# Summing the modulation vectors by 32x32 turns on VectorE and one small matmul, with the w_mod tiles in three buffers

## The chip, the cores and the metric

The kernel runs on one core of one Trainium2 chip. The metric is the device time of one execution in microseconds (us). A core has several engines that work side by side: TensorE (matrix products; PE in the profile, PEld its loading of weights), VectorE (DVE), ScalarE (ACT), GpSimd (POOL) and SyncE (SP), whose queue here issues all the DMA transfers from the main memory to the core's own.

## The reference

Two layers work on 256 latent tokens and 256 context tokens of width 1024. What matters here is the modulation: each layer makes six vectors of 1024 numbers out of the conditioning vector, once for the latent tokens (from c) and, where they are still needed, once for the context tokens (from c_ctx).

```
mod   = silu(c)     @ w_mod[l] + b_mod[l]
mod_c = silu(c_ctx) @ w_mod[l] + b_mod[l]
sh1, sc1, gt1, sh2, sc2, gt2 = split(mod, 6)
...
h = rms_norm(x, g_norm1) * (1 + sc1) + sh1          # then w_in, three mixers, three gates
x = x + gt1 * (merged branches @ w_o)
x = x + gt2 * (square(relu((rms_norm(x, g_norm2) * (1 + sc2) + sh2) @ w_ff1)) @ w_ff2)
```

w_mod[l] is 1024 x 6144 numbers of 4 bytes. It is as large a matrix as the others, but it is multiplied by two vectors only.

## The kernel before

**The main work.** All activations lie with the feature on the partition. Every big matrix comes from memory in tiles of 1 MB (`ffL_raw`, `gateL_raw` and so on, two buffers). ScalarE rounds a tile to its high part (`whi`, L384), VectorE computes the low part (`wlo`, L385), and TensorE multiplies in three passes: high by high (L473), low by high (L476) and high by low (L478). In the feed-forward part of layer 1 the same three passes stand in L1110 to L1112. The stages of a layer follow each other: norm 1, u, conv, Fourier, qkv, gate (with the attention beside it), ag, wo, ff.

**The modulation beside it.** At the start, shift and scale of norm 1 of layer 0 are computed by TensorE (`mod_start`). All other vectors are made in the background by a generator, `mod_steps`, whose list holds (layer, vector j, number of streams): four vectors with two streams in layer 0, two with two streams in layer 1, four with one stream in layer 1. For each half of a vector (512 columns) it asks for four tiles of w_mod of 512 KB (`modr`, L298: 256 rows x 512 columns, two row blocks of 128). For each row block and stream VectorE does one step: it multiplies the 128 x 512 block by the conditioning numbers of these 128 rows, one for each partition, and adds the product to an accumulator `acc` (L349 for the first, L351 for the others). After 16 steps two accumulators are full: either the same half for both streams, or both halves for one stream.

**The finish.** Each accumulator then still has to be summed over its 128 partitions, and the sums have to be turned so that the feature lies on the partition. That is `mod_finish`, and it is called 16 times: 8 for the four vectors of layer 0, 4 for the two first ones of layer 1, 4 for the last ones. Before the change it does, for each pair of accumulators:

- three empty steps (W1), then four matmuls of 32 equal rows of ones by 256 columns of an accumulator (L308); each puts 256 sums on 32 partitions of one PSUM tile, all 32 rows alike
- a copy of that 128 x 256 tile to SBUF by ScalarE (L313)
- two empty steps (W2), then two 128 x 128 transposes by TensorE (L318) to a PSUM tile of the kind `aux`, which the attention uses too
- two additions of the bias by VectorE (L321), which write the vectors to `modT`

**What sets the order.** `fm`, the function of the three passes, calls `mods.tick()` after each of its 128-row blocks of the contraction. A tick adds the stage's rate (RATES: 0.6 in gate, 1.3 in ag, 0.4 in wo, 0.8 in ff), and each time a whole step is due, one step of the generator is written into the program. `mod_need` writes at once all steps that are left until a vector is ready: before wo for vectors 2, 3 and 4 of layer 0, and in the first block of ff for vector 5. `mods.drain` writes all that is left before the last projection of layer 0. The instructions of the modulation are pinned among each other by `keep_in_program_order`; the others are put in order for each engine by a scheduler that simulates the timeline when the program is built. An instruction with no pin can so be placed ahead of others that were written before it, once its buffer is free. Each engine then takes its list strictly in order.

**The start.** Two tiles of the kind `modr` serve at first as a place for weights of `w_in` (`start_raw`, L501); the first w_mod tile of the generator comes when one of them is free.

Of the kernel before, what the change touches and what calls it, by code (L numbers as in the profile page):

```python
# [1 line left out]

# [6 lines left out]
F32 = mybir.dt.float32  # L9
F32R = mybir.dt.float32r  # L10
AF = mybir.ActivationFunctionType
ALU = mybir.AluOpType
AX = mybir.AxisListType
PSUM = bass.MemoryType.PSUM

P = 128
D = 1024
# [13 lines left out]
W_INIT, W_RMS = 6, 6  # L31
MLAG = 1
LAG = 2
W1, W2 = 3, 2
RATES = [0.6, 1.3, 0.4, 0.8]
AR = [1.3, 0.8]

# [2 lines left out]
def hybrid_block_kernel(  # L40
# [7 lines left out]
    nc = tc.nc  # L48
    V = nc.vector
    A = nc.scalar  # L50
    G = nc.gpsimd
    PE = nc.tensor

    const = ctx.enter_context(tc.tile_pool(name="const", bufs=1))
# [4 lines left out]
    tiny = ctx.enter_context(tc.tile_pool(name="tiny", bufs=4))  # L59
    psum = ctx.enter_context(tc.tile_pool(name="psum", bufs=4, space=PSUM))  # L60
    paux = ctx.enter_context(tc.tile_pool(name="paux", bufs=3, space=PSUM))
    pmod = ctx.enter_context(tc.tile_pool(name="pmod", bufs=1, space=PSUM))
# [4 lines left out]
    def nm(s):  # L67
        uid[0] += 1
        return f"{stage[0]}_{s}_{uid[0]}"
# [4 lines left out]
    def scratch(shape=(P, 512), dt=F32):  # L74
        return scr.tile(list(shape), dt, tag="scr", name=nm("scr"))

    def small(shape, tag, dt=F32, bufs=4):
        return tiny.tile(shape, dt, tag=tag, name=nm(tag), bufs=bufs)

    def bank(shape=(P, 512)):  # L80
        return psum.tile(list(shape), F32, tag="mm", name=nm("mm"))

    def aux(shape=(P, 512)):
        return paux.tile(list(shape), F32, tag="aux", name=nm("aux"))

    def raw_tile():
        return rpool.tile([P, 2048], F32, tag="raw", name=nm("raw"))

    class Ring:
# [6 lines left out]
        def next(self):  # L96
            self.i += 1
            return self.t[:, self.lo + self.i % self.n, :]
# [31 lines left out]
    ident = const.tile([P, P], F32, tag="ident", name="ident")  # L130
    make_identity(nc, ident)
    ones = const.tile([P, P], F32, tag="ones", name="ones")
    G.memset(ones, 1.0)
    mhalf = const.tile([P, 1], F32, tag="mhalf", name="mhalf")
    G.memset(mhalf, -0.5)
    cT = scratch((P, KT, 32))
# [10 lines left out]
    prm = []  # L147
# [38 lines left out]
    def accs(streams):  # L186
        t = const.tile([P, 4, 512], F32, tag="kT", name=nm("acc"))[:, 0, :]
        return [Acc(s * S, S, t) for s in streams]
# [62 lines left out]
    modT = [const.tile([P, 48, 2], F32, tag=f"modT{l}", name=f"modT{l}") for l in range(DEPTH)]  # L251
# [40 lines left out]
    def mod_loads(todo):  # L292
        for l, j, ns in todo:
            for h in range(2):
                for k2 in range(KT // 2):
                    r = tiny.tile([P, 2, 512], F32, tag="modr", name=nm("modr"), bufs=2)
                    c0 = j * D + h * 512
                    nc.sync.dma_start(r, w_mod[l, k2 * 256 : (k2 + 1) * 256, c0 : c0 + 512]  # L298
                                      .rearrange("(k p) n -> p k n", p=P))
                    yield l, j, ns, h, k2, r  # L300

    def mod_finish(accs, dsts, l):

        ps = pmod.tile([P, 256], F32, tag="mod", name=nm("mod"))
        for _ in range(W1):
            yield
        for g in range(4):
            tc.keep_in_program_order(PE.matmul(  # L308
                ps[32 * g : 32 * g + 32, :], ones[:, 0:32],
                accs[g // 2][:, (g % 2) * 256 : (g % 2 + 1) * 256], start=True, stop=True,  # L310
            ))
        sb = scratch()[:, :256]
        A.copy(sb, ps)  # L313
        for _ in range(W2):
            yield
        tp = aux((P, 2, P))
        for e in range(2):
            tc.keep_in_program_order(PE.transpose(tp[:, e, :], sb[:, e * P : (e + 1) * P], ident))  # L318
        tv = tp.rearrange("p e (g r) -> p g e r", r=32)[:, :, :, 0]
        for i, (f, s) in enumerate(dsts):  # L320
            V.tensor_tensor(  # L321
                modT[l][:, f : f + 4, s].rearrange("p (g e) -> p g e", e=2),
                tv[:, 2 * i : 2 * i + 2, :],
                prm[l][:, f : f + 4].rearrange("p (g e) -> p g e", e=2), op=ALU.add,
            )
        yield

    ready = set()
# [4 lines left out]

    def mod_steps(todo):
        loads = mod_loads(todo)
        cur = next(loads, None)
        accs, dsts = [], []
        while cur is not None:
            l, j, ns, h, k2, r = cur
            cur = next(loads, None)  # L340
            if k2 == 0:
                for s in range(ns):
                    accs.append(small([P, 512], "acc", bufs=2))
                    dsts.append((j * 8 + h * 4, s))
            for kk in range(2):
                for s in range(ns):
                    a, w = accs[s - ns], cs2[:, s, 2 * k2 + kk : 2 * k2 + kk + 1]
                    if k2 + kk == 0:
                        v = V.tensor_scalar(a, r[:, kk, :], w, None, op0=ALU.mult)  # L349
                    else:  # L350
                        v = V.scalar_tensor_tensor(a, r[:, kk, :], w, a, op0=ALU.mult, op1=ALU.add)  # L351
                    tc.keep_in_program_order(v)
                    yield
            if k2 == KT // 2 - 1 and len(accs) == 2:
                yield from mod_finish(accs, dsts, l)
                accs, dsts = [], []
                if h == 1:
                    ready.add((l, j))
# [129 lines left out]
    def residual(f, ps, gt, streams, acc):  # L488
        for s in streams:
# [5 lines left out]
            if acc is not None:  # L495
# [2 lines left out]

    start_raw = [raw_tile(), raw_tile()]
    start_raw = [[r[:, i * 1024 : (i + 1) * 1024] for i in range(2)] for r in start_raw]  # L500
    start_raw.append([tiny.tile([P, D], F32, tag="modr", name=nm("modr"), bufs=2)  # L501
                      for _ in range(2)])

    def start_weights(i):
# [41 lines left out]
    for l in range(DEPTH):  # L546
        last = l == DEPTH - 1
        ns = 1 if last else 2
# [15 lines left out]
        if l == 0:  # L564
# [31 lines left out]
            for i in range(3):  # L596
                go(KT - 1, i, i + 1)
            mods.set(mod_steps(
                [(0, j, 2) for j in range(2, 6)] + [(1, 1, 2), (1, 0, 2)]
                + [(1, j, 1) for j in range(2, 6)]  # L600
# [15 lines left out]
        for ft in range(2):  # L616
            t = scratch()
# [15 lines left out]
        for ft in range(2):  # L633
# [4 lines left out]
            t = scratch()  # L638
# [31 lines left out]
        for tt in range(nt):  # L670
            ps = aux((P, 2, 256))
# [17 lines left out]
        for ft in range(2):  # L689
            ps = aux()  # L690
# [111 lines left out]
        for ci, c0 in ((2, OFF_K), (0, OFF_Q), (1, OFF_Q + 256)):  # L802
            ch = plain(w_in[l], 0, c0, (V, G) if last else (V, V)).prep()
            for tt in range(4 if ci == 2 else nt):
                ps = bank((P, 256))
                tk = slice(tt * P, (tt + 1) * P)
                for kt in range(KT):
                    wh, wl = ch.at(kt, 0, 256)
                    a, b = hh[:, kt, tk], hl[:, kt, tk]
# [122 lines left out]
        for j in range(4):  # L932
# [5 lines left out]
            for o in range(2):  # L938
                f = 2 * j + o
# [42 lines left out]
        acc = accs(streams)  # L982
# [50 lines left out]
        for b in range(nblk):  # L1033
            subs = []
            hot = None
            for q in range(2):
                hid = bigt([P, 2, per, T])
                subs.append(hid)
                for j in range(per // 2):
# [12 lines left out]
                    for o in range(2):  # L1052
                        t = scratch()[:, :T]
# [20 lines left out]
            if nr == 1:  # L1074
                if final and not last:
                    mods.drain()
                    acc = accs(streams)
# [17 lines left out]
            else:  # L1095

                nk = 2 * per
                for h in range(2):
# [14 lines left out]
                    for tt in range(2):  # L1113
                        t = scratch()
# [51 lines left out]
```

## Time and profile before

| what | value |
|---|---|
| three timed runs | 1146.95, 1144.39, 1149.06 us; median 1146.95 us |
| the profiled execution | 1148.35 us, its span 1146.5 us |
| granted TensorE clock | 0.996 |
| VectorE busy | 779.6 us (68%) |
| ScalarE busy | 504.4 us (44%) |
| DMA, all queues | 180.03 MB, 157 GB/s on the mean |

The span runs from the first to the last instruction; 1.85 us of the execution lie around it. A group of instructions is shown with its line, its engine, its operation, what it writes and reads, its shape and count; then its busy time, the mean of one in ns, and the engine's idle time before it with what ended it. In the timeline each row has a start and a length in us, and equal neighbours are merged. The length of a matmul is longer than the distance to the next one, because matmuls are pipelined: what one costs is read from the distances of the starts. A TensorE product of plain 4-byte numbers stands as two records, one of its transposes as one.

### The profile page before, as it was taken

The numbers are of one execution on the slowest core, as the hardware profiler recorded it, in microseconds if no ns is written. First come the engines' busy times: TensorE is split into PE (matmuls) and PEld (weight loads), VectorE is DVE, ScalarE is ACT, GpSimd is POOL, SyncE is SP. The second block draws the span as 40 slices with busy tenths as digits, with TensorE's granted clock in tenths as the row PEclk, the third lists the DMA queues.
The fourth block names the chain that finished last, engine by engine and source line by source line (L and its number), as shares of the span: only waits on it lengthen the run. The fifth ranks groups of instructions, "written<-read, shape, count | busy, mean of one in ns | idle before, by whom it ended". The sixth has DMA issues, their size and how long they took to land.

```text
span 1146.5 us, 17789 instructions
## 1 busy us (share of the span) xinstructions
PE 1127.0 (98%) x7075; PEld 983.9 (86%) x7075; DVE 779.6 (68%) x1444; ACT 504.4 (44%) x896; POOL 50.6 (4%) x54
## 2 busy tenths in 40 slices
PE   7899999999999999999999999999999999999998
PEld 6689887887787998878888888899999999988986
DVE  4577775568878876766746664778886567756754
ACT  4345544443332454143134135244666456754752
POOL 0002100000000100000000000043300000000000
PEclk9999999999999999999999999999999999999999
DMA  9933322225655243655456664515434465656653
GB/s 279 295 97 100 107 78 92 82 85 147 202 175 179 91 162 117 196 184 165 146 168 202 217 209 145 199 61 175 139 111 129 131 207 178 184 182 186 184 184 111
DMA packets 156796, 180.03 MB, mean 157 GB/s; under 512 B 5260, under 2 KB 126504, under 8 KB 156712
## 3 DMA queue, kind: packets, MB, share of 16 engines
q1 hardware_dynamic: 156712, 178.88, 50.1%
q8 instruction: 56, 0.92, 0.3%
q14 instruction: 28, 0.23, 0.1%
HBM read 177.81 MB, written 1.05 MB: 156 GB/s over the span
## 4 chain that ended last, share of the span: by engine, by line
PE 88%; DVE 4%; DMA 4%; SPq 2%; ACT 1%; issue 1%; POOL 1%; DVEq 0%; ACTq 0%; POOLq 0%
PE ffL_mm L473 12%; PE ffL_mm L476 12%; PE ffL_mm L478 12%; PE gateL_mm L478 5%; PE gateL_mm L473 5%; PE gateL_mm L476 5%; PE agL_mm L476 3%; PE agL_mm L473 3%; PE agL_mm L478 3%; PE ffL_mm L1112 3%; PE ffL_mm L1111 3%; PE ffL_mm L1110 3%; PE woL_mm L476 2%; PE woL_mm L478 2%; PE woL_mm L473 2%; SPq L105 2%
## 5 line engine op out<-in xcount | busy, mean ns | idle before, releaser
L384 ACT CAST ffL_whi<-ffL_raw 128x1024 fp32r<-128x1024 f32 x128 | 134.4, 1052 | 218.9 <-PE ffL_mm L478 164.3
L385 DVE TENSOR_TENSOR ffL_wlo<-ffL_raw,ffL_whi 128x1024 fp32r<-128x1024 f32 x127 | 155.0, 1222 | 99.3 <-ACT ffL_whi L384 99.1
L473 PE MATMUL ffL_mm<-woL_big,ffL_whi 128*128 128x258 f32 (+2 forms) x544 | 171.0, 329 | 0.0
L476 PE MATMUL ffL_mm<-woL_big,ffL_wlo 128*128 128x258 f32 (+2 forms) x544 | 170.5, 327 | 0.0
L478 PE MATMUL ffL_mm<-woL_big,ffL_whi 128*128 128x258 f32 (+2 forms) x544 | 133.2, 328 | 0.0
L473 PEld LDWEIGHTS ffL_mm<-woL_big,ffL_whi 128*128 128x128 f32 x544 | 103.1, 190 | 10.2 <-issue 1.6
L476 PEld LDWEIGHTS ffL_mm<-woL_big,ffL_wlo 128*128 128x128 f32 x544 | 103.1, 190 | 8.9 <-issue 0.4
L351 DVE SCALAR_TENSOR_TENSOR ffL_acc<-ffL_modr,cs,ffL_acc 128x512 f32<-128x512 f32 x126 | 90.4, 747 | 24.4 <-DMA ffL_modr<-in_w_mod_dram 23.4
L473 PE MATMUL ffL_mm<-ffL_big,ffL_whi 128*128 128x512 f32 (+1 forms) x288 | 105.4, 368 | 0.0
L476 PE MATMUL ffL_mm<-ffL_big,ffL_wlo 128*128 128x512 f32 (+1 forms) x288 | 104.9, 367 | 0.0
L478 PEld LDWEIGHTS ffL_mm<-woL_big,ffL_whi 128*128 128x128 f32 x544 | 91.0, 190 | 8.7
L478 PE MATMUL ffL_mm<-ffL_big,ffL_whi 128*128 128x512 f32 (+1 forms) x288 | 85.1, 367 | 0.0
L473 PEld LDWEIGHTS ffL_mm<-ffL_big,ffL_whi 128*128 128x128 f32 x288 | 54.3, 189 | 10.6 <-issue 2.1
L476 PEld LDWEIGHTS ffL_mm<-ffL_big,ffL_wlo 128*128 128x128 f32 x288 | 54.3, 189 | 9.1 <-issue 0.4
L385 DVE TENSOR_TENSOR gateL_wlo<-gateL_raw,gateL_whi 128x1024 fp32r<-128x1024 f32 x40 | 48.8, 1221 | 19.3 <-ACT gateL_whi L384 19.1
L478 PEld LDWEIGHTS ffL_mm<-ffL_big,ffL_whi 128*128 128x128 f32 x288 | 53.2, 189 | 8.7
L384 ACT CAST gateL_whi<-gateL_raw 128x1024 fp32r<-128x1024 f32 x40 | 42.0, 1051 | 22.0 <-PE gateL_mm L478 18.2
L476 PE MATMUL gateL_mm<-n1L_big,gateL_wlo 128*128 128x512 f32 x128 | 50.7, 396 | 0.0
L473 PE MATMUL gateL_mm<-n1L_big,gateL_whi 128*128 128x512 f32 x128 | 50.5, 396 | 0.0
L1110 PE MATMUL ffL_mm<-ffL_whi,ffL_big 128*128 128x512 f32 x128 | 49.9, 390 | 0.0
L1111 PE MATMUL ffL_mm<-ffL_wlo,ffL_big 128*128 128x512 f32 x128 | 49.8, 389 | 0.0
L1112 PE MATMUL ffL_mm<-ffL_whi,ffL_big 128*128 128x512 f32 x128 | 49.8, 389 | 0.0
(339 smaller groups left out, 2626.8 us busy)
## 6 DMA issues: line engine op xcount, KB each, us to landing
ffL_raw<-in_w_ff_dram SPq DMA_DIRECT2D x64, 1024.0 KB, 5.5
ffL_modr<-in_w_mod_dram SPq DMA_DIRECT2D x53, 512.0 KB, 4.3
gateL_raw<-in_w_in_dram SPq DMA_DIRECT2D x16, 1024.0 KB, 5.3
init_big<-in_w_mod_dram SPq DMA_DIRECT2D x16, 512.0 KB, 7.8
agL_raw<-in_w_in_dram SPq DMA_DIRECT2D x8, 1024.0 KB, 5.4
woL_raw<-in_w_o_dram SPq DMA_DIRECT2D x8, 1024.0 KB
qkvL_raw<-in_w_in_dram SPq DMA_DIRECT2D x6, 1024.0 KB
agL_modr<-in_w_mod_dram SPq DMA_DIRECT2D x11, 512.0 KB, 5.1
```

Of the source, the lines that this page charges most:

```text
L105: tc.keep_in_program_order(nc.sync.dma_start(dst, src))
L351: v = V.scalar_tensor_tensor(a, r[:, kk, :], w, a, op0=ALU.mult, op1=ALU.add)
L384: a = A.copy(hi[:, :n], src)
L385: b = eng.tensor_tensor(lo[:, :n], src, hi[:, :n].bitcast(F32), op=ALU.subtract)
L473: m = PE.matmul(d, wh, rh, start=kt == first, stop=False)
L476: PE.matmul(d, wl, rh, start=False, stop=False)
L478: PE.matmul(d, wh, rl, start=False, stop=kt == final)
L1110: PE.matmul(bs[tt], hid[:, 0], wh, start=kk == 0, stop=False)
L1111: PE.matmul(bs[tt], hid[:, 0], wl, start=False, stop=False)
L1112: PE.matmul(bs[tt], hid[:, 1], wh, start=False, stop=kk == nk - 1)
```

## The change

The finish no longer uses TensorE for the sums of 256 columns and for the transposes. VectorE turns each 128 x 512 accumulator in blocks of 32 x 32 (`V.transpose`), so that the column within a block lies on the partition, and then sums over the free axis within each block (`V.reduce_sum`, 512 numbers to 16). What is left is a sum over the four groups of 32 partitions. One matmul does it with a constant `sel` (128 x 128, a one wherever row and column agree modulo 32), which is built at the start by two VectorE instructions. Its moving side has 32 columns. Four additions of the bias, each on 32 partitions, then write to `modT` straight from its PSUM tile. The empty steps before the matmul become two, those before the transposes go, and the two pairs of VectorE instructions stand each in one step. Each finish so takes 5 steps of the generator in place of 6 beside its 16 steps of summing.

Besides, the w_mod tiles lie in three buffers, and the generator asks for a tile two tiles ahead of its use.

```diff
-W1, W2 = 3, 2
+W1 = 2
...
+    sel = const.tile([P, P], F32, tag="sel", name="sel")
+    quad = small([P, 32], "quad", bufs=1)
+    V.reduce_sum(quad, ident.rearrange("p (g c) -> p c g", c=32), axis=AX.X)
+    V.tensor_copy(sel.rearrange("p (g c) -> p g c", c=32), quad.unsqueeze(1).to_broadcast([P, 4, 32]))
...
-                    r = tiny.tile([P, 2, 512], F32, tag="modr", name=nm("modr"), bufs=2)
+                    r = tiny.tile([P, 2, 512], F32, tag="modr", name=nm("modr"), bufs=3)
...
-        ps = pmod.tile([P, 256], F32, tag="mod", name=nm("mod"))
+        red = small([P, 2, 16], "red", bufs=2)
+        for i, acc in enumerate(accs):
+            t = scratch()
+            tc.keep_in_program_order(V.transpose(t, acc))
+            tc.keep_in_program_order(
+                V.reduce_sum(red[:, i], t.rearrange("p (b r) -> p b r", r=32), axis=AX.X))
+            yield
         for _ in range(W1):
             yield
+        ps = pmod.tile([P, 2, 16], F32, tag="mod", name=nm("mod"))
+        tc.keep_in_program_order(PE.matmul(
+            ps.rearrange("p i b -> p (i b)"), sel, red.rearrange("p i b -> p (i b)"),
+            start=True, stop=True))
+        (f, s0), (_, s1) = dsts
         for g in range(4):
-            tc.keep_in_program_order(PE.matmul(
-                ps[32 * g : 32 * g + 32, :], ones[:, 0:32],
-                accs[g // 2][:, (g % 2) * 256 : (g % 2 + 1) * 256], start=True, stop=True,
-            ))
-        sb = scratch()[:, :256]
-        A.copy(sb, ps)
-        for _ in range(W2):
-            yield
-        tp = aux((P, 2, P))
-        for e in range(2):
-            tc.keep_in_program_order(PE.transpose(tp[:, e, :], sb[:, e * P : (e + 1) * P], ident))
-        tv = tp.rearrange("p e (g r) -> p g e r", r=32)[:, :, :, 0]
-        for i, (f, s) in enumerate(dsts):
-            V.tensor_tensor(
-                modT[l][:, f : f + 4, s].rearrange("p (g e) -> p g e", e=2),
-                tv[:, 2 * i : 2 * i + 2, :],
-                prm[l][:, f : f + 4].rearrange("p (g e) -> p g e", e=2), op=ALU.add,
-            )
+            q = slice(32 * g, 32 * g + 32)
+            src = ps[q].rearrange("p i (c g) -> p i c g", g=4)[:, :, :, g]
+            if s1 != s0:
+                dst = modT[l][q, f : f + 4, :].rearrange("p c i -> p i c")
+                bias = prm[l][q, f : f + 4].unsqueeze(1).to_broadcast([32, 2, 4])
+            else:
+                dst = modT[l][q, f : f + 8, s0].rearrange("p (i c) -> p i c", c=4)
+                bias = prm[l][q, f : f + 8].rearrange("p (i c) -> p i c", c=4)
+            V.tensor_tensor(dst, src, bias, op=ALU.add)
         yield
...
-        cur = next(loads, None)
+        ahead = [next(loads) for _ in range(2)]
         accs, dsts = [], []
-        while cur is not None:
-            l, j, ns, h, k2, r = cur
-            cur = next(loads, None)
+        while ahead:
+            l, j, ns, h, k2, r = ahead.pop(0)
+            ahead.extend(islice(loads, 1))
...
-    start_raw.append([tiny.tile([P, D], F32, tag="modr", name=nm("modr"), bufs=2)
+    start_raw.append([tiny.tile([P, D], F32, tag="modr", name=nm("modr"), bufs=3)
```

More of the change, by code (lines that the diff above doesn't have):

```diff
@@ L1 @@
 from contextlib import ExitStack
+from itertools import islice
 import concourse.bass as bass
@@ L1153 @@
     from concourse.bass_utils import run_bass_kernel_spmd as run
-    nc = bacc.Bacc("TRN2", target_bir_lowering=False, num_devices=1)
+    nc = bacc.Bacc("TRN2", target_bir_lowering=False, num_devices=1, dynamic_dma_scratch_size=1024)
     arrays, args = {}, []
```

## Prediction

> **What bounds the kernel now.** I read the page first, then the waits of TensorE, then the timeline around one finish. On the page the first line and the chain name the engine.
>
> ```profile
> PE 1127.0 (98%) x7075; PEld 983.9 (86%) x7075; DVE 779.6 (68%) x1444; ACT 504.4 (44%) x896; POOL 50.6 (4%) x54
> PE 88%; DVE 4%; DMA 4%; SPq 2%; ACT 1%; issue 1%; POOL 1%; DVEq 0%; ACTq 0%; POOLq 0%
> ```
>
> A busy TensorE alone proves little, since a matmul's row is longer than the distance to the next. The waits of TensorE show that it hardly stands still after the start. The rows for the start are the longest, and of all waits of the finishes one is left:
>
> ```profile
> PE init_aux L151 <- DMA init_scr<-in_w_conv_dram: 3.3, 1, 3.3
> ...
> PE ffL_mod L308 <- DVE ffL_acc L351: 0.4, 1, 0.4
> ```
>
> So from the first stages to the end the kernel is TensorE's queue, and what leaves that queue leaves the time, as long as nothing else becomes late.
>
> **What a finish costs on TensorE.** The timeline of one finish in the feed-forward part:
>
> ```profile
> 549.58 0.61 PE L478 MATMUL ffL_mm<-ffL_big,ffL_whi 128*128 128x512 f32 x2
> 550.13 0.64 PE L308 MATMUL ffL_mod<-ffL_acc,ones 128*32 128x256 f32 x8
> 550.70 0.50 PE L473 MATMUL ffL_mm<-ffL_big,ffL_whi 128*128 128x512 f32 x1
> 551.03 0.39 PE L476 MATMUL ffL_mm<-ffL_big,ffL_wlo 128*128 128x512 f32 x1
> ...
> 555.37 0.40 PE L473 MATMUL ffL_mm<-ffL_big,ffL_whi 128*128 128x512 f32 x1
> 555.61 0.38 PE L318 MATMUL ffL_aux<-ident,ffL_scr 128*128 128x128 f32 x2
> ...
> 556.06 0.63 PE L478 MATMUL ffL_mm<-ffL_big,ffL_whi 128*128 128x512 f32 x2
> ```
>
> Two equal neighbours merged last 0.61 to 0.63, one lasts 0.39: a 512-column matmul starts some 0.225 us after its forerunner. Without the four L308 matmuls (eight records), L476 would start at 549.58 + 3 x 0.225 = 550.26; it starts at 551.03. They cost 0.77 us, much of it before and after their own rows. Without the two transposes, L478 would start at 555.37 + 2 x 0.225 = 555.82; it starts at 556.06: 0.24 us.
>
> Where the schedule splits the four matmuls in two pairs, each pair pays that again. The neighbours here have 256 columns and 0.12 us of distance:
>
> ```profile
> 370.02 0.28 PE L476 MATMUL woL_mm<-agL_big,woL_wlo 128*128 128x256 f32 x1
> 370.23 0.62 PE L308 MATMUL woL_mod<-woL_acc,ones 128*32 128x256 f32 x4
> 370.78 0.50 PE L478 MATMUL woL_mm<-agL_big,woL_whi 128*128 128x256 f32 x2
> 371.12 0.28 PE L473 MATMUL woL_mm<-agL_big,woL_whi 128*128 128x256 f32 x1
> ```
>
> 370.02 + 3 x 0.12 = 370.38 against 371.12: 0.74 us for a pair. Along the timeline ten of the 16 finishes go in one block of eight records like the first, and six in blocks of four like the second (one of these among attention matmuls, taken at one block's price): 10 x 0.77 + 5 x 1.48 + 0.77 = 15.9 us. The transposes make 16 x 0.24 = 3.8 us. **Removed from TensorE: 19.7 us.**
>
> **What the new matmul costs there.** It has two records, loads 128 weight columns and moves 32. No row has that shape, but rows on either side of it have, with one column and with 128:
>
> ```profile
> 395.34 0.52 PE L478 MATMUL ffL_mm<-woL_big,ffL_whi 128*128 128x256 f32 x3
> 395.70 0.50 PE L203 MATMUL woL_aux<-ones,woL_acc 128*128 128x1 f32 x4
> 396.07 0.36 PE L473 MATMUL ffL_mm<-woL_big,ffL_whi 128*128 128x256 f32 x1
> 396.27 0.28 PE L476 MATMUL ffL_mm<-woL_big,ffL_wlo 128*128 128x256 f32 x1
> ```
>
> ```profile
> 389.74 0.28 PE L478 MATMUL woL_mm<-agL_big,woL_whi 128*128 128x256 f32 x1
> 389.86 0.61 PE L218 MATMUL woL_aux<-woL_scr,ones 128*128 128x128 f32 x4
> 390.23 0.36 PE L473 MATMUL woL_mm<-agL_big,woL_whi 128*128 128x256 f32 x1
> 390.43 0.28 PE L476 MATMUL woL_mm<-agL_big,woL_wlo 128*128 128x256 f32 x1
> ```
>
> By the same subtraction, two matmuls with one column cost 396.27 - (395.34 + 4 x 0.12) = 0.45 us, and two with 128 columns 390.43 - (389.74 + 2 x 0.12) = 0.45 us. The columns moved don't matter in that range, so one matmul costs 0.225 us, or at most 0.45 if it pays alone what two pay together; it has two records as the transposes have, which paid 0.24. I take 0.23: 16 x 0.23 = 3.7 us (bounds 1.8, if the half of it is hidden as nothing here shows, and 7.2). **Net on TensorE: -16.0 us.**
>
> The Trainium skill (VectorE: DVE Perf Modes, The three transpose paths and Rules for kernel authors) speaks against the move: a 128x128 transpose belongs on TensorE, and it gives 390 ns there against 311 on VectorE for a bf16 tile. By these figures (an estimate) the 32 transposes would be worth 12.5 us on TensorE, and 32 turns of four such blocks would cost VectorE 40 us; TensorE's rows give 3.8 us for the former, and no run here shows the latter yet.
>
> **What VectorE takes on.** Per finish two turns and two sums of 128x512, and four small additions in place of two. Nearest rows, and the row that shows how VectorE instructions follow each other:
>
> ```profile
> L837 DVE TENSOR_REDUCE gateL_mx<-gateL_aux 128x1 f32<-128x512 f32 x32 | 21.8, 683 | 9.7 <-PE gateL_aux L834 9.6
> L538 DVE COPY xT<-init_mm 128x512 f32<-128x512 f32 x4 | 2.7, 689 | 0.6 <-PE init_mm L534 0.6
> L349 DVE TENSOR_SCALAR ffL_acc<-ffL_modr,cs 128x512 f32<-128x512 f32 x18 | 8.2, 480 | 6.7 <-DMA ffL_modr<-in_w_mod_dram 6.4 <-PE ffL_mod L308 0.2
> L321 DVE TENSOR_TENSOR modT<-ffL_aux,prm 128x4 f32<-128x4 f32 x20 | 2.3, 156 | 13.8 <-PE ffL_aux L318 13.8
> ```
>
> ```profile
> 336.83 4.06 DVE L351 SCALAR_TENSOR_TENSOR agL_acc<-agL_modr,cs,agL_acc 128x512 f32<-128x512 f32 x6
> ```
>
> Four instructions of 683 to 689 ns make 2.7 us, two more small ones of 156 ns 0.3 us: 3.0 us a finish. In a row they overlap a little (six L351 take 4.06 us, 0.68 each), so 3.0 is the generous price; the turn is bounded below by 0.48 (L349, the quickest 128x512 row) and above, as no row shows a turn, by two passes, 1.4. All 16 finishes: 48 us, between 40 and 70.
>
> VectorE in the stretch from 290 to 375 us (its busy time, with the number of instructions; the granted clock, the DMA's share and rate):
>
> ```profile
> 290.00:375.00 85.00, 68.53 (x109) 1.00 0.60 187
> ```
>
> In the feed-forward stages, where ten finishes lie, VectorE has room and I cost this at nothing: the cover is the idle third of VectorE's time on the page. The tight place is 290 to 375 us, ag and the head of wo, where the rate is 1.3 and `mod_need` writes the rest of vector 4 at once: VectorE is busy 68.5 of 85 us, and four finishes lie in it. They add 12 us: 80.5 of then 82 us (TensorE saves four times some 0.8). Queued behind the new instructions there are the low parts (L385) and the gating that frees PSUM banks, and TensorE waits for both. Two tiles of low parts and one group of banks are ahead, which takes up delays of a few us. If all the present idle time is used the price is 0; if none of it can be (it is waiting for TensorE's results), TensorE pays what was added less what its own queue lost there, 12 - 4 x 0.8 = 9 us. I take 1.0 us, nearer to none, since TensorE shows no wait there now.
>
> ScalarE loses 16 copies; it isn't late anywhere, so this is worth 0. The four matmuls that waited 0.4 us for VectorE at the end of layer 0 are gone, but the new one waits for four more VectorE instructions there: 0.
>
> **The third buffer.** VectorE now waits for w_mod tiles, in the row of L349 above and in this one:
>
> ```profile
> DVE ffL_acc L351 <- DMA ffL_modr<-in_w_mod_dram: 23.4, 16, 3.8
> ```
>
> Most of these 30 us should go. That is worth 0 by itself, as TensorE waited for that chain only the 0.4 us. What the free buffer triggers is at the start. The first w_mod tile of the generator waits now until a start tile is used up; with a third buffer nothing holds it, and it carries no pin. SP's queue, a row of the chain of waits and the rate of the DMA by slices of 28.7 us:
>
> ```profile
> 5.78 1.88 SPq L105 DMA_DIRECT2D init_big<-in_ctx_dram  x2
> 11.57 0.93 SPq L105 DMA_DIRECT2D init_raw<-in_w_in_dram  x2
> ```
>
> ```profile
> 30.60 7.55 DMA init_big<-in_w_mod_dram
> ```
>
> ```profile
> GB/s 279 295 97 100 107 78 92 82 85 147 202 175 179 91 162 117 196 184 165 146 168 202 217 209 145 199 61 175 139 111 129 131 207 178 184 182 186 184 184 111
> ```
>
> SP has nothing to issue between 7.7 and 11.6 us, so the scheduler can put the tile there. The start is a chain of transfers (that at 30.60 is on it), and 512 KB more at 279 to 295 GB/s push it back by up to 1.9 us; some of it may fall in the hole before 11.6. If the tile stays behind the start's, the price is 0. I take 1.0. The two instructions that build `sel` on VectorE (128x128 each, at most 0.7 us by L837) hide in the same start.
>
> **The sum** against the profiled execution, 1148.35 us (span 1146.5 and 1.85 around it): -19.7 + 3.7 + 1.0 + 1.0 = -14.0, so 1134.35. That execution stands 1.4 us above the median of the three runs, 1146.95; from there it is 1132.95, so 1133.0.
>
> **The rivals.** *A, the sum holds:* 1133.0.
>
> *B, VectorE becomes the bound in ag and wo.* For it speak the 80.5 of 82 us, and that the turn's price is unknown; against it that the generator then has less left for `mod_need` (a finish has 5 steps in place of 6). Price: up to 9 us in place of 1, and the full 1.9 at the start: 1146.95 - 16.0 + 9 + 1.9 = 1142.
>
> *C, the matmul waits at the head of TensorE's queue.* It comes after two turns and two sums, and everything behind it in TensorE's list waits with it. The distance in the list comes from the scheduler's simulation; if that holds a turn or a sum for much shorter than it is, TensorE stands still in each finish for up to VectorE's 2.7 us and what is in front of them there. Against it speaks the margin now, in VectorE's and TensorE's timeline:
>
> ```profile
> 482.41 3.40 DVE L351 SCALAR_TENSOR_TENSOR ffL_acc<-ffL_modr,cs,ffL_acc 128x512 f32<-128x512 f32 x5
> 490.20 0.64 PE L308 MATMUL ffL_mod<-ffL_acc,ones 128*32 128x256 f32 x8
> ```
>
> The last step ends at 485.8 and the matmul comes 4.4 us later, more than 2.7. The point from which it decides is a mean wait of 16.0 / 16 = 1.0 us a finish; at 2.7 it gives 1146.95 - 16.0 + 43 + 1 = 1175, slower.
>
> *D, no change: the end of layer 0 is set by the loads.* The chain passes there from TensorE to w_mod tiles:
>
> ```profile
> 727.26 7.81 DMA ffL_modr<-in_w_mod_dram
> ```
>
> If that chain ran by its own clock, what TensorE gained in the 15 finishes before it would be lost there, 15 x 1.0 = 15 us, and the time would be 1146. Against it: the tiles are asked for when VectorE frees a buffer, and VectorE keeps pace with TensorE's order, not with a clock; and the third buffer shortens just this. The Trainium skill (Perfetto Trace Analysis, Identifying the Most-Contended Engine) would have TensorE judged by its weight loads and not by its matmuls' rows: by it TensorE is at 86% here, not 98%, and has room, which would favour D. The rows of TensorE's waits say otherwise.
>
> **How the numbers follow.** A 0.72, B 0.16, C 0.06, D 0.06. About 0.5%, 5.7 us, can be told from no change here, so faster means under 1141.2. All of A and two thirds of B lie there: 0.82. The rest of B and D are the same: 0.12. C is slower: 0.06. The range reaches below to the sum without the prices at the start and in ag (1131), with the new matmul at half its price (1129) and 2 us for the scatter of the runs before: 1127. Above it takes in B: 1142.
>
> **What would show it.** Right: eight L308 records and two L318 gone at each finish, one matmul of two records with 0.2 to 0.25 us in its place; TensorE's waits as short as before; VectorE some 48 us busier than 779.6; the `modr` waits far below 30 us. Wrong: a turn far over 0.7 us; TensorE's rows with waits for `red` or for low parts in ag and wo; an L298 issue before 12 us and the first matmuls later by 2 us or more.

## The result and the profile after

| what | before | changed |
|---|---|---|
| timed runs, median | 1145.67 us (1143.88 to 1149.06) | 1134.19 us (1132.81 to 1136.58) |
| ratio of the times, with its 95% interval | | 0.9899 [0.9866, 0.9931] |
| the profiled execution | 1148.35 us, span 1146.5 | 1135.44 us, span 1133.7 |

The kernel became 11.5 us faster; the forecast was 1133.0 us. The diff above does not show two lines of the change: an import, and `dynamic_dma_scratch_size=1024`, with which the program is built. No run has this line alone; the experiment with buffers only has it too and was slower than before, so the gain does not come from it. One run of all, at 1382.89 us and a granted clock of 0.748, was slow; it is one of the ten of the kernel with the rate 0.5 and does not count in its ratio.

The page of the changed kernel, its busy times and the chain:

```profile
PE 1111.1 (98%) x6947; PEld 983.5 (87%) x6947; DVE 825.9 (73%) x1542; ACT 498.2 (44%) x880; POOL 49.8 (4%) x54
PE 92%; DMA 3%; SPq 2%; DVE 1%; ACT 1%; POOL 0%; issue 0%; ACTq 0%; DVEq 0%
```

VectorE is 46.3 us busier (forecast 48), and TensorE holds still more of the chain. Its waits, in total, times, longest:

```profile
PE n1L_mm L484 <- ACT n1L_big L246: 3.7, 2, 3.5
PE init_aux L157 <- DMA init_scr<-in_w_conv_dram: 3.4, 1, 3.4
...
PE gateL_aux L860 <- DVE qkvL_big L854: 1.7, 1, 1.7
...
PE gateL_aux L860 <- ACT qkvL_big L862: 0.8, 1, 0.8
```

None is for `red`. But three stand out as longer than before or new: one at the start (2.5 us in all before) and two in the attention. One finish on TensorE:

```profile
542.05 0.62 PE L489 MATMUL ffL_mm<-ffL_big,ffL_whi 128*128 128x512 f32 x2
542.51 0.30 PE L323 MATMUL ffL_mod<-ffL_red,sel 128*128 128x32 f32 x2
542.64 0.48 PE L484 MATMUL ffL_mm<-ffL_big,ffL_whi 128*128 128x512 f32 x1
542.96 0.39 PE L487 MATMUL ffL_mm<-ffL_big,ffL_wlo 128*128 128x512 f32 x1
```

Without L323, L487 would start at 542.05 + 3 x 0.227 = 542.73; it starts at 542.96. The new matmul costs 0.23 us. VectorE's part of that finish:

```profile
525.76 1.30 DVE L316 STREAM_TRANSPOSE ffL_scr<-ffL_acc 128x512 f32<-128x512 f32 x2
526.99 0.64 DVE L318 TENSOR_REDUCE ffL_red<-ffL_scr 128x16 f32<-128x512 f32 x1
527.55 1.21 DVE L396 TENSOR_TENSOR ffL_wlo<-ffL_raw,ffL_whi 128x1024 fp32r<-128x1024 f32 x1
528.68 0.68 DVE L318 TENSOR_REDUCE ffL_red<-ffL_scr 128x16 f32<-128x512 f32 x1
...
543.57 0.69 DVE L336 TENSOR_TENSOR modT<-ffL_mod,prm 32x8 f32<-32x8 f32 x4
```

A turn takes 0.65 us, about as long as a sum, and the matmul comes 13 us after the last sum. All `modr` waits of VectorE together have shrunk from 33.2 us to 3.5. The largest group that is left (its idle time stands behind the bar):

```profile
L362 DVE SCALAR_TENSOR_TENSOR ffL_acc<-ffL_modr,cs,ffL_acc 128x512 f32<-128x512 f32 x126 | 90.4, 748 | 3.8 <-DMA ffL_modr<-in_w_mod_dram 2.7
```

And VectorE in the stretch called tight, 290 to 375 us (68.53 us busy before):

```profile
290.00:375.00 85.00, 83.06 (x137) 1.00 0.65 196
```

**Where the time went.** All kernels here run the same 5868 matmuls of the three passes. So the start of the n-th of them is compared with before's n-th (its 401st, 1201st, 1673rd, 3234th and the last), and each stretch of before's profile gets its gain or loss. The other columns are the experiments below, one profiled execution each; all in us:

| stretch of before | finishes | changed | turns only | buffers only | no turns | changed, again | tiles held, again |
|---|---|---|---|---|---|---|---|
| to 105 (start) | | +0.71 | -3.93 | -0.17 | -1.03 | -0.20 | -3.62 |
| 105 to 316 (gate, attention) | 3 | +0.26 | -0.20 | +0.86 | -3.07 | -1.37 | -1.62 |
| 316 to 402 (ag, wo) | 3 | -3.88 | -3.88 | +0.02 | -3.86 | -3.88 | -3.88 |
| 402 to 745 (ff) | 10 | -9.28 | -9.28 | +1.44 | -9.24 | -9.28 | -9.28 |
| 745 to the end | | -0.60 | -0.32 | -0.31 | +0.19 | -0.43 | -0.79 |
| sum | | -12.79 | -17.61 | +1.84 | -17.01 | -15.16 | -19.19 |

The rows of ag, wo and ff are as good as equal wherever the old finish is gone: the gain is there. What the kernels differ in lies ahead of 316 us, and part of it is a stretch of halved clock, which some of the profiles have and some do not (below, at the last pair of runs).

### The profile page after: what moved, and what is told of

Read it like the earlier page. It is cut to its first block, busy times and chain, and to the rows that moved or that the text cites. A ratio compares the mean times of both kernels' runs of the same rounds, so it can differ in the third digit from the quotient of the medians.

```text
span 1133.7 us, 17600 instructions
## 1 busy us (share of the span) xinstructions
PE 1111.1 (98%) x6947; PEld 983.5 (87%) x6947; DVE 825.9 (73%) x1542; ACT 498.2 (44%) x880; POOL 49.8 (4%) x54
## 4 chain that ended last, share of the span: by engine, by line
PE 92%; DMA 3%; SPq 2%; DVE 1%; ACT 1%; POOL 0%; issue 0%; ACTq 0%; DVEq 0%
PE ffL_mm L484 13%; PE ffL_mm L489 13%; PE ffL_mm L487 13%; PE gateL_mm L484 5%; PE gateL_mm L489 5%; PE gateL_mm L487 5%; PE agL_mm L489 3%; PE agL_mm L484 3%; PE agL_mm L487 3%; PE ffL_mm L1121 3%; PE ffL_mm L1123 3%; PE ffL_mm L1122 3%; PE woL_mm L484 2%; PE woL_mm L489 2%; PE woL_mm L487 2%; SPq L106 2%
## 5 line engine op out<-in xcount | busy, mean ns | idle before, releaser
L487 PE MATMUL ffL_mm<-woL_big,ffL_wlo 128*128 128x258 f32 (+2 forms) x544 | 170.4, 327 | 0.0
L487 PEld LDWEIGHTS ffL_mm<-woL_big,ffL_wlo 128*128 128x128 f32 x544 | 103.1, 190 | 8.6
L487 PE MATMUL ffL_mm<-ffL_big,ffL_wlo 128*128 128x512 f32 (+1 forms) x288 | 104.7, 366 | 0.0
L487 PEld LDWEIGHTS ffL_mm<-ffL_big,ffL_wlo 128*128 128x128 f32 x288 | 54.3, 189 | 8.6
L487 PE MATMUL gateL_mm<-n1L_big,gateL_wlo 128*128 128x512 f32 x128 | 50.4, 394 | 0.0
```

Of the source, the lines that this page charges most:

```text
L487: PE.matmul(d, wl, rh, start=False, stop=False)
```

## The experiments

The theory: some 16 us leave TensorE's queue, the turns cost it nothing, and the third buffer brings nothing by itself and costs at the start. The rivals: VectorE's added work takes some us back in gate, ag or wo; the buffers bring part of the gain. Before ran beside each group on the same chip: median 1145.88 us for the first four kernels, 1147.39 for the next four, 1145.86 for the last four. Where a kernel has several runs, its time is followed by its ratio to before and the 95% interval.

**Turns only**: the changed kernel with two buffers and one tile asked for ahead.

```diff
-                    r = tiny.tile([P, 2, 512], F32, tag="modr", name=nm("modr"), bufs=3)
+                    r = tiny.tile([P, 2, 512], F32, tag="modr", name=nm("modr"), bufs=2)
...
-    start_raw.append([tiny.tile([P, D], F32, tag="modr", name=nm("modr"), bufs=3)
+    start_raw.append([tiny.tile([P, D], F32, tag="modr", name=nm("modr"), bufs=2)
...
-        ahead = [next(loads) for _ in range(2)]
+        ahead = [next(loads) for _ in range(1)]
```

> The new finish with the old two w_mod buffers and one tile of lookahead. Theory (all of the gain is TensorE's queue): the span is 12 to 14 us shorter than before's 1146.5, as short as the changed kernel's 1133.7 or up to 1 us shorter, since the extra tile at the start is gone (its shift was 0.7 us); VectorE's waits for w_mod tiles come back to about 25 to 35 us and cost nothing. Rival (the third buffer carries part of the gain, at the end of layer 0 where the chain of before ran over w_mod tiles): 8 to 11 us shorter than before only, with TensorE waiting for VectorE between 700 and 745 us.

Measured: 1130.75 us, 0.9868 [0.9839, 0.9898]. VectorE waits for the tiles again, and nobody minds:

```profile
DVE ffL_acc L362 <- DMA ffL_modr<-in_w_mod_dram: 23.4, 13, 4.2
DVE ffL_acc L360 <- DMA ffL_modr<-in_w_mod_dram: 5.4, 2, 2.9
```

The turns alone bring the whole gain and, by the medians, 2 to 3 us more than the change (1134.19 us, and 1132.9 when it was measured again). The span is 17.6 us under before's, where the theory had 12 to 14: the start gained 3.9 us by itself.

**Buffers only**: the old finish, three buffers, two tiles ahead (and the line of the scratch size).

```diff
-        cur = next(loads, None)
...
+        ahead = [next(loads) for _ in range(2)]
```

> The old finish with three w_mod buffers and two tiles of lookahead. Theory: VectorE's waits for w_mod tiles fall from 33 us to under 8 us and the span does not get shorter: 0 to 1.5 us longer than before's 1146.5, by the extra tile ahead of the conv weights at the start. Rival (the buffers carry part of the gain): 2 us or more shorter.

Measured: 1148.35 us, 1.0024 [1.0011, 1.0037]: slower by 2.5 us, where the theory had 0 to 1.5. The `modr` waits fell to 14.1 us only (theory: under 8), and the longest of the finishes' waits on TensorE grew from 0.4 us:

```profile
PE ffL_mod L309 <- DVE ffL_acc L352: 1.8, 1, 1.8
```

So the third buffer brought none of the gain.

**No turns**: the changed kernel without turns and sums.

```diff
-            t = scratch()
-            tc.keep_in_program_order(V.transpose(t, acc))
-            tc.keep_in_program_order(
-                V.reduce_sum(red[:, i], t.rearrange("p (b r) -> p b r", r=32), axis=AX.X))
+            tc.keep_in_program_order(V.tensor_copy(red[:, i], acc[:, 0:16]))
```

> The changed kernel with the turns and the sums of the finish left out: each pair is replaced by a copy of 128x16 numbers, so the modulation vectors are not the reference's. VectorE has some 37 us less to do. Theory 1 (the gain that is missing in the gate stage, some 3 us between 240 and 280 us, is VectorE's new work in front of the attention's): span 1130 to 1131. Theory 2 (it comes from the order in which the scheduler put TensorE's list, whatever VectorE needs): within 1 us of 1133.7. Rival B of the prediction (VectorE also costs time in ag and wo): 1128 or less.

Measured: 1131.14 us, 0.9868 [0.9844, 0.9892]. From 105 us on it gains 3.07 + 3.86 + 9.24 - 0.19 = 15.98 us. In ag, wo and ff that equals the kernels with turns, so there the turns are free. In gate it is 3.3 us better than the changed kernel. By its span, 1129.5 us, theory 1 (VectorE's work) looks right for gate; the gate stretch of the kernel with the matmul four times, shown with the last pair of runs, speaks for theory 2.

**Tiles held**: the changed kernel, with the first three w_mod tiles of the generator pinned behind the transfers written before them.

```diff
-                    nc.sync.dma_start(r, w_mod[l, k2 * 256 : (k2 + 1) * 256, c0 : c0 + 512]
-                                      .rearrange("(k p) n -> p k n", p=P))
+                    dma = nc.sync.dma_start(r, w_mod[l, k2 * 256 : (k2 + 1) * 256, c0 : c0 + 512]
+                                            .rearrange("(k p) n -> p k n", p=P))
+                    if (l, j, h) == (0, 2, 0) and k2 < 3:
+                        tc.keep_in_program_order(dma)
```

> The changed kernel with the first three w_mod tiles of the generator pinned behind the transfers written before them, so that none of them is issued before about 76 us. Theory (two tiles ahead of the conv weights delay the start): the conv weights land up to 2.4 us earlier than the changed kernel's 57.0 us and the first stages end 0.7 to 1.4 us earlier, span 1132.0 to 1133.0. Rival (the start is set by the chain through ScalarE and VectorE, not by that transfer): no change, 1133.7.

Measured: 1129.76 us, 0.9859 [0.9831, 0.9887]. What the third buffer costs is the place of its first tiles. The changed kernel's SyncE, ScalarE and TensorE at the start (in square brackets the idle time before and what ended it):

```profile
44.33 2.21 SPq L304 DMA_DIRECT2D gateL_modr<-in_w_mod_dram  x2
47.94 0.37 SPq L434 DMA_DIRECT2D convL_raw<-in_w_in_dram  x1
```

```profile
57.13 1.04 ACT L395 CAST convL_whi<-convL_raw 128x1024 fp32r<-128x1024 f32 x1 [9.44 <-DMA convL_raw<-in_w_in_dram]
58.08 0.90 ACT L246 ACTIVATE n1L_big<-n1L_scr,modT 128x256 fp32r<-128x256 f32 x2
```

```profile
59.03 0.55 PE L484 MATMUL n1L_mm<-n1L_big,n1L_whi 128*128 128x512 f32 x1 [3.50 <-ACT n1L_big L246]
```

Two w_mod tiles stand ahead of the conv weights. ScalarE's list has the rounding of these weights ahead of the activations that TensorE waits for, so the late transfer stops all three. With the tiles held:

```profile
52.78 1.05 ACT L397 CAST convL_whi<-convL_raw 128x1024 fp32r<-128x1024 f32 x1 [5.78 <-DMA convL_raw<-in_w_in_dram]
53.74 0.90 ACT L246 ACTIVATE n1L_big<-n1L_scr,modT 128x256 fp32r<-128x256 f32 x2
```

TensorE's matmuls then follow without a wait, from 54.79 us on, and the granted clock from 52 to 66 us is 1.00, in the changed kernel 0.88. The start gained more than the theory had: 5.6 us against the changed kernel's first profile, 3.4 us in the repeated pair below. In the other kernels with two tiles ahead that row of ScalarE starts at 55.2 to 56.3 us, in those with the tiles held at 52.8 to 54.1.

**Turns twice**: the changed kernel, each turn and each sum issued twice.

```diff
-            tc.keep_in_program_order(V.transpose(t, acc))
+            for _ in range(2):
+                tc.keep_in_program_order(V.transpose(t, acc))
```

(and the sum likewise)

> The changed kernel with each turn and each sum done twice: VectorE has some 40 us more to do. Theory (VectorE has room in all stages but the attention of layer 0): from 316 us on TensorE's distances are those of the changed kernel within 1 us, and all that is lost, 0 to 5 us, is lost before that. Rival B (ag and the head of wo are at VectorE's bound): 3 us or more lost between 290 and 375 us alone.

Measured, one run: 1148.57 us, 13 us more than the changed kernel's profiled run. Against that the stretches gave +0.2 at the start, +1.1 in gate, +8.8 in ag and wo, +1.9 in ff, +1.0 behind. There TensorE now waits for VectorE's sum, and twice for ScalarE:

```profile
PE agL_mod L325 <- DVE agL_red L320: 3.0, 1, 3.0
PE woL_mm L486 <- ACT agL_scr L911: 1.7, 1, 1.7
PE agL_mm L486 <- ACT agL_scr L911: 1.7, 1, 1.7
```

So the theory (all lost ahead of 316 us) failed at double the load, and rival C is real there: 3.0 us once, followed by 3.4 us at half the clock (granted 0.50 from 361.1 to 364.5 us). The loss in ag and wo has the place and the size of rival B. But the two waits of 1.7 us are for ScalarE's gating, and one like them stands also in each of three kernels below whose VectorE does each turn once (rate 0.5, split steps, no empty steps). How much of the 8.8 us is VectorE's load alone is not shown. The busy share would not have told: VectorE in 311 to 363 us, first of the changed kernel, then of this one:

```profile
311.00:363.00 52.00, 51.13 (x82) 1.00 0.61 186
```

```profile
311.00:363.00 52.00, 50.80 (x83) 0.98 0.53 168
```

Both are full; one costs TensorE nothing, the other 8.8 us.

**Matmul four times**: the changed kernel, the matmul of the finish issued four times.

```diff
+        for _ in range(4):
             tc.keep_in_program_order(PE.matmul(
```

> The changed kernel with the small matmul done four times in place of once in each finish. Theory (two records of 0.11 us each, as the rows with one and with 128 columns had): 3 x 0.22 x 16 = 10.7 us longer than the changed kernel, 0.65 to 0.70 us in each finish of the feed-forward part. Rival (most of the 0.23 us is the break in the stream, paid once): 3 to 5 us longer.

Measured, one run: 1141.9 us. In ff its ten finishes gain 2.42 us in place of 9.28, 0.69 us each for three more matmuls: 0.23 each.

```profile
463.02 0.62 PE L490 MATMUL ffL_mm<-ffL_big,ffL_whi 128*128 128x512 f32 x2
463.47 0.97 PE L324 MATMUL ffL_mod<-ffL_red,sel 128*128 128x32 f32 x8
464.28 0.48 PE L485 MATMUL ffL_mm<-ffL_big,ffL_whi 128*128 128x512 f32 x1
464.60 0.39 PE L488 MATMUL ffL_mm<-ffL_big,ffL_wlo 128*128 128x512 f32 x1
```

464.60 - (463.02 + 3 x 0.227) = 0.90 us for eight records; two cost 0.23. In all the kernel is 6.5 us longer than the changed kernel's profiled run, where the theory had 10.7. The 13 finishes of ag, wo and ff cost 8.9 us more, close to the 13 x 0.66 = 8.6 of the theory; the start was 0.6 us shorter and gate 1.5, although three finishes lie in gate.

**Tiles held, other rates**: the kernel with the tiles held, and another rate of the generator in gate. I thought that gate's loss came from a finish that meets the end of the attention, so that a finish a little earlier or later would avoid it.

```diff
-RATES = [0.6, 1.3, 0.4, 0.8]
+RATES = [0.7, 1.3, 0.4, 0.8]
```

> The kernel with the held w_mod tiles and a rate of 0.7 in place of 0.6 in the gate stage, so that the second finish comes at three quarters of that stage and not with the attention's last blocks. Theory (the 2.4 us lost between 256 and 285 us come from that meeting): 2 us shorter than with the held tiles alone, a span of about 1126, without TensorE's 1.7 us wait for the attention's scaling. Rival (any finish inside the attention costs the same): 1128, no change.

Measured: 1136.45 us, 0.9916 [0.9895, 0.9937]. Gate became 5.7 us slower than in before's profile, with a new wait in the attention and 6.8 us of halved clock around it (granted 0.50 from 242.6 to 249.4 us):

```profile
PE gateL_aux L862 <- DVE gateL_rs L855: 2.1, 1, 2.1
```

And with a rate below the change's:

```diff
-RATES = [0.6, 1.3, 0.4, 0.8]
+RATES = [0.5, 1.3, 0.4, 0.8]
```

> The same with a rate of 0.5, so that the second finish comes after the attention and more steps are left for ag and for the burst ahead of wo. Theory: 2 us shorter than with the held tiles alone, about 1126, as VectorE has room in ag. Rival B: what is gained in the attention is lost between 290 and 375 us, 1128 or more.

Measured: 1144.8 us, 0.9983 [0.9968, 0.9999]. Gate gained 1.2 us; the two profiles of the held kernel gained 0.1 and 1.6. The steps left over pile up before wo, where TensorE waits for norm 2, and then has half its clock from 387.3 to 400.9 us:

```profile
PE woL_aux L209 <- DVE woL_acc L189: 6.4, 1, 6.4
```

With the rate of 0.5 the two waits at the end of the attention are gone, but two others, of 0.7 and 0.9 us, come at 200 us. Another rate moved the waits and did not remove them, and neither kernel became quicker.

**Split steps**: the tiles held, the turn and the sum each in a step of its own, one empty step.

```diff
             tc.keep_in_program_order(V.transpose(t, acc))
+            yield
...
-W1 = 2
+W1 = 1
```

> The held tiles, and the turn and the sum of an accumulator each in a step of its own, with one empty step less (a finish then has six steps, as before the change). Theory (the attention's scaling loses because two or four of VectorE's new instructions stand together in front of it): the 2.4 us lost between 256 and 285 us shrink to under 1, span 1126 to 1127. Rival (it is the order that the scheduler finds, whatever the length of the wedge): no gain, or a loss in another place; 1128 or more.

Measured: 1132.33 us, 0.9873 [0.9849, 0.9896]. Between 256 and 285 us nothing is lost any more, but the waits of 0.7 and 0.9 us at 200 us are here too, and gate as a whole gained 1.2 us. Between 316 and 402 us the gain shrank from 3.9 to 0.3 us; TensorE waited there 1.7 us once for ScalarE and 0.6 us for VectorE, and no wait shows the rest. So the loss moved to other places, as the rival had it.

**No empty steps**: the changed kernel without the steps between the last sum and the matmul.

```diff
-W1 = 2
+W1 = 0
```

> The changed kernel without empty steps between the sums and the small matmul. Theory (rival C does not happen because the scheduler puts the matmul where it expects the sums to be done): no wait of TensorE for the sums over 0.5 us, and the time within 3 us of the changed kernel's, the difference being order in the attention. Rival C: TensorE waits for the sums, up to 2.5 us in each of 16 finishes, 1150 or more.

Measured, one run: 1135.18 us, beside 1135.44 for the changed kernel's profiled run. TensorE never waits for `red`, even with no step between. In ag, wo and ff the gains are those of the changed kernel to 0.11 us.

**The changed kernel again, and the tiles held again**, side by side on one chip, no edit beyond the above.

> The changed kernel once more, beside the next two on the same chip, since the start of the executions scatters. Theory (the third buffer costs 2 to 4 us at the start, where the generator's tiles go ahead of the conv weights): 1132 to 1135, 11 to 14 us under before, and 3 to 5 us above the kernel with the held tiles. Rival (that difference was the scatter of single executions): the two agree within 1.5 us.

> The kernel with the held w_mod tiles once more. Theory: 1128 to 1131, its conv weights land by 54 us and TensorE has no wait of 2 us or more before the first matmuls of that stage. Rival: within 1.5 us of the changed kernel.

Measured: 1132.9 us, 0.9882 [0.9861, 0.9904], and 1129.05 us, 0.9843 [0.9819, 0.9868]. With the tiles held it is 3.9 us quicker than the change and the best version found.

This pair of runs of the changed kernel also shows what in gate comes from where. The end of the attention on TensorE, in the first profile:

```profile
267.21 0.44 PE L860 MATMUL gateL_aux<-ident,qkvL_big 128*128 128x128 f32 x2 [0.80 <-ACT qkvL_big L862]
269.32 0.41 PE L860 MATMUL gateL_aux<-ident,qkvL_big 128*128 128x128 f32 x2 [1.66 <-DVE qkvL_big L854]
269.66 1.24 PE L872 MATMUL gateL_aux<-qkvL_big,qkvL_vt 128*64 128x128 f32 x16
270.82 0.69 PE L484 MATMUL gateL_mm<-convL_big,gateL_whi 128*128 128x512 f32 x1
271.31 0.63 PE L487 MATMUL gateL_mm<-convL_big,gateL_wlo 128*128 128x512 f32 x1
271.74 0.63 PE L489 MATMUL gateL_mm<-convL_big,gateL_whi 128*128 128x512 f32 x1
```

And in the second, with the same lists:

```profile
266.30 0.44 PE L860 MATMUL gateL_aux<-ident,qkvL_big 128*128 128x128 f32 x2 [0.80 <-ACT qkvL_big L862]
268.40 0.41 PE L860 MATMUL gateL_aux<-ident,qkvL_big 128*128 128x128 f32 x2 [1.66 <-DVE qkvL_big L854]
268.74 1.24 PE L872 MATMUL gateL_aux<-qkvL_big,qkvL_vt 128*64 128x128 f32 x16
269.90 0.50 PE L484 MATMUL gateL_mm<-convL_big,gateL_whi 128*128 128x512 f32 x1
270.24 0.39 PE L487 MATMUL gateL_mm<-convL_big,gateL_wlo 128*128 128x512 f32 x1
270.47 0.40 PE L489 MATMUL gateL_mm<-convL_big,gateL_whi 128*128 128x512 f32 x1
```

The waits are equal to 0.01 us. After them the matmuls start 0.43 us apart in the first and 0.23 in the second. The granted clock (after the number of instructions) of the 3.5 us from that point, first profile, then second:

```profile
270.80:274.30 3.50, 3.50 (x10) 0.52 0.51 157
```

```profile
269.90:273.40 3.50, 3.50 (x16) 1.00 0.55 159
```

Eight distances take 3.48 us in one and 1.95 in the other: 1.5 of the 1.63 us by which the two differ in this stretch. The rest of gate's loss, 3.07 - 1.37 = 1.7 us, is in both. It goes with the two waits, 2.46 us together, which neither before nor the kernel without turns has. The halved clock stands also in the profiles of turns only and of the first kernel with the tiles held, behind waits of 0.5 and 1.7 us at this place (gate -0.20 and -0.09), but not in the second (-1.62), which has the same waits. VectorE ahead of them, in the first profile:

```profile
265.85 1.22 DVE L396 TENSOR_TENSOR agL_wlo<-agL_raw,agL_whi 128x1024 fp32r<-128x1024 f32 x1 [1.95 <-ACT agL_whi L395]
267.00 0.42 DVE L848 TENSOR_REDUCE gateL_mx<-gateL_aux 128x1 f32<-128x256 f32 x1
...
268.82 0.35 DVE L854 TENSOR_SCALAR qkvL_big<-qkvL_big,gateL_rs 128x256 f32<-128x256 f32 x1
```

There is no turn in it: the attention's maximum stands behind a low part of ag, which waited 1.95 us for ScalarE. The turns reach TensorE here by the order into which the scheduler put the rest. The kernel with the matmul four times bears this out. It has all the turns and sums, and VectorE is as busy in the stretch from 105 to 316 us (157.3 us, in the changed kernel 156.4), but there the maximum stands ahead of the low part:

```profile
264.89 0.42 DVE L849 TENSOR_REDUCE gateL_mx<-gateL_aux 128x1 f32<-128x256 f32 x1 [2.36 <-PE gateL_aux L846]
...
268.21 0.70 DVE L316 STREAM_TRANSPOSE gateL_scr<-gateL_acc 128x512 f32<-128x512 f32 x1
268.84 1.18 DVE L397 TENSOR_TENSOR agL_wlo<-agL_raw,agL_whi 128x1024 fp32r<-128x1024 f32 x1
```

TensorE has one wait of 0.2 us or more left in its attention:

```profile
PE gateL_aux L873 <- ACT qkvL_big L863: 0.2, 1, 0.2
```

Gate gained 1.2 us with three finishes that each cost 0.69 us more; without this it is 3.3, as much as without turns (3.1). So VectorE's added work is free in gate too, in the order that this kernel has.

## Why the prediction was right

- **Removed 19.7, new matmul 3.7, net -16.0 us.** Right, and by the steps given: 0.23 us for the matmul (0.69 for three more); 15.98 us from 105 us on where the turns are left out. It holds by stretches too. A finish in one block is worth 0.77 + 0.24 - 0.23 = 0.78 us, one in two blocks 1.48 + 0.24 - 0.23 = 1.49. Before's trace has eleven of the first kind and five of the second (the one among the attention's matmuls, counted with the six but priced as one block, is one block). Ag and wo have one and two: 3.8 us, measured 3.88. Ff has nine and one: 8.5, measured 9.28; the nine gave 0.81 each, and the split one 1.97, with 0.4 us of its wait.
- **VectorE 3.0 us a finish, 48 in all.** 46.3. The turn, bounded by 0.48 and 1.4, is 0.65 us. The estimate from the Trainium skill (VectorE: DVE Perf Modes, The three transpose paths), 40 us for the turns, came out twice too high: 32 x 0.65 = 21.
- **ag and wo +1.0, rival B.** Zero. VectorE was as full there as forecast, and the gain in this stretch is the same with and without turns. At double the load this stretch lost 8.8 us; where between the two B would begin, and how much of the loss is B, stays open.
- **Rival C.** No wait for `red` in the changed kernel, nor without the empty steps; 3.0 us once at double load.
- **Rival D.** Wrong: ff gave all of its gain, also with two buffers and 30 us of `modr` waits. The prediction was right to go by TensorE's waits. Its weight loads were busy for 86% of the span before and 87% after, and still what left its queue left the time: the room that the prediction read out of the rule of the Trainium skill (Perfetto Trace Analysis, Identifying the Most-Contended Engine) was not there.
- **Start +1.0.** The size was near in the profiled pair, +0.71; the place was wrong. No w_mod tile was issued in SP's pause before 12 us. Two tiles went out at 44.3 us ahead of the conv weights, and the price came through ScalarE's list. It is larger than forecast if measured against the same kernel with the tiles held: 3.9 us by the medians, more than the 1.9 that the prediction took as the most. Before's profile had part of it already (a wait of 2.3 us at that place), with one tile ahead, and the kernel with turns only had none of it, also with one tile ahead (0.6 us). Why these two differ stays open.
- **Not in the sum: gate.** 1.7 us by two waits in the attention, and up to 1.6 more by the clock after them. The prediction looked for VectorE's price only where VectorE is fullest. That the waits come from the scheduler's order and not from VectorE's time is shown by the kernel with the matmul four times, which has the same work of VectorE and none of the two waits. No kernel sets that order by hand with all else equal.

The profiled pair gained 12.8 us where 14.0 were forecast: a right main term, less the price in ag and wo that did not come, and with 1.7 to 3.3 us in gate that nobody had asked for. The 16 us were worked out. That the rest took 3.2 us of it, near the 2.0 that were forecast, is luck: neither price stood where it was looked for, and 1.5 us hang on a halved clock that the next profile of the same kernel did not have.

## What to carry to other kernels

When one engine's queue is the time, price a change by the distances of the starts in that queue, row by row, with the split blocks counted apart; in ff it held to 0.03 us a finish for the nine in one block. A full engine beside it costs nothing until the rows show the bound engine waiting for it, so look for waits and not for shares. An extra buffer on a path that nobody waits for buys nothing, but its first transfers can stand ahead of one that is waited for: find what stands behind them in the queue, and pin them.

## What the runs showed of the hardware

- After a wait TensorE may run at half its clock for some 3.5 us: 0.43 us between 512-column matmuls in place of 0.23, granted clock 0.52 to 0.6. It came after waits of 2.06 to 3.5 us at the start, and after two waits of 2.2 to 2.5 us together in gate in some profiles (changed, turns only, tiles held) and not in others with the same waits (both of the repeated pair). The Trainium skill (TensorE: Matmul & The Clock Gate, Part 1: The HAM clock gate) says that the clock is halved after an idle window of about 3.4 us, and that the windows run freely, so that runs of one kernel differ. The halving and the difference between runs agree; here a wait of 2.06 us, six tenths of such a window, was enough. In the profile's pages of before and of the changed kernel the row of the clock in 40 slices shows nines throughout, so this is seen only in rows and short stretches.
- A turn of 128 x 512 4-byte numbers in blocks of 32 x 32 takes VectorE 0.65 to 0.70 us, as long as a sum over the same block.
- A 4-byte matmul between 512-column ones costs 0.23 us with 32 columns, where the prediction had 0.225 for one column and for 128 (between 256-column ones): in this range the columns don't count.
